# Weights of a hybrid decoder trunk, laid out in the order in which the kernel reads them

## The chip, the cores and the metric

The kernel runs on one core of one Trainium2 chip. The metric is the device time of one execution in microseconds (us); the number to beat is the median of several runs.

## The reference

Two layers, each a conditioned mixer over a sequence of 1024 tokens of width 1024, all in float32. The conditioning vector `c` is turned into shift, scale and gate by `w_mod`; the normalised and modulated input goes through one wide projection `w_in`, whose columns feed three groups of heads (sliding-window attention, retention, gated linear attention); the gated results are joined and go through `w_out`.

```python
def hybrid_layer(x, c_act, positions, w_mod, b_mod, pre_gain, post_gain, w_in, sinks,
                 gla_gate_w, gla_gate_b, gla_norm_gain, w_out):
    mod = c_act @ w_mod + b_mod                      # w_mod: 1024 x 3072
    shift, scale, gate = jnp.split(mod[:, None, :], 3, axis=-1)
    h = rms_norm(x, pre_gain) * (1.0 + scale) + shift
    proj = h @ w_in                                  # w_in: 1024 x 3088
    (aq, ak, av, ag, rq, rk, rv, rg, gq, gk, gv, gg, ga) = jnp.split(proj, IN_SPLITS, axis=-1)
    ...
    y = jnp.concatenate([a_out, r_out, g_out], axis=-1) @ w_out   # w_out: 1024 x 1024
    return x + gate * rms_norm(y, post_gain)
```

## The kernel before

The sequence lies in eight tiles of 128 tokens. The projections run in float32 accuracy as three passes over a high and a low part of each operand, so every weight block is loaded once and then split into two tiles: the high part by a copy (ScalarE, ACT, or VectorE, DVE) and the low part by a subtraction (DVE or GpSimd, POOL). The split is what the lines 529 to 535 do, under the names `arena<-st` in the profile.

**Weights of the projections.** `w_in` is cut into 12 units of 256 columns (`gg`, `rg`, `rq`, `rk`, `rv`, `gqk`, `gv`, `kv`, `aq0`, `aq1`, `ag0`, `ag1`), `w_out` of layer 0 into four (`o0` to `o3`). `load(l, name)` fetches a unit in four transfers: each brings, for 128 partitions, two pieces of 256 columns (1 KB each) into one of five `st` buffers (256 KB). The contraction index of such a piece is `(k p)`: partition p of piece k is row 128 k + p of the weight, so neighbouring partitions read neighbouring rows. With the unit `gg` go the 16 columns `ga`, in one transfer of 64 KB made of pieces of 64 bytes (line 541). For layer 1's output the four units are replaced by blocks of 128 x 512, loaded by `sw_load` in one piece of 2 KB per partition.

**Weights of the conditioning.** `mod_first` computes shift and scale of layer 0 at the very start: for each half of the columns (`hh`) it loads two tiles `wm` of 8 x 512 columns per partition, one for shift (summed by TensorE, PE) and one for scale (summed by DVE, line 328), in transfers of two, two, two, one and one `k`. Here the contraction index is `(p k)`: partition p has rows 8 p to 8 p + 7. All other thirds are done by `mod_third`, one transfer of 128 x 512 for each k (line 361), in the same `st` buffers.

**The order of the work.** PE's order is written out by the source: generators are queued as jobs and released against a planned clock `clk[0]` with due times from the table `L`; this planned clock does not look at the layout of a transfer. For the other engines and the DMA queues the order of instructions is settled when the kernel is built (line 1703 leaves only PE to the source). Every engine then runs its list in order. Nearly all weight transfers are issued from SyncE's queue (SP). The x tiles of the first two tokens' tiles (`xk`) are issued from ACT's queue, the next two (`mx`) from SP after the second half's `wm`, the later ones (`pre_first`, `t<-in_x`) after that; constants come with `cload` (line 234), called below them in the source.

The host side, `kernel()`, already permutes columns of `w_in` and rows of `w_out`.

Of the kernel before, what the change touches and what calls it, by code (L numbers as in the profile page):

```python
# [17 lines left out]
P = 128  # L18
D = 1024
S = 1024  # L20
DEPTH = 2
NT = S // P
NP_ = NT // 2
KT = D // P
# [4 lines left out]
GQ, GK, GV, GG, GA = 2304, 2432, 2560, 2816, 3072  # L29
D_IN = 3088  # L30

UNITS = [
    ("gg", GG), ("rg", RG),
    ("rq", RQ), ("rk", RK), ("rv", RV),
    ("gqk", GQ), ("gv", GV),
    ("kv", AK), ("aq0", AQ), ("aq1", AQ + 256),
    ("ag0", AG), ("ag1", AG + 256),
    ("o0", 0), ("o1", 256), ("o2", 512), ("o3", 768),
]
COLS = dict(UNITS)  # L40

LOG_CLAMP = -24.0

# [48 lines left out]
def trunk(ctx: ExitStack, tc: tile.TileContext, ins, cst, out):  # L92
    nc = tc.nc
    V, A, G, T = nc.vector, nc.scalar, nc.gpsimd, nc.tensor
    x_in, c_in, pos_in, w_mod, b_mod, pre_g, post_g, w_in, sinks, gw_in, gb_in, gn_in, w_out = [
        ins[n] for n in _INS
    ]

# [21 lines left out]
    def small(w, dt=F32):  # L120
        return gp.tile([P, w], dt, tag="sm", name=nm("sm"), bufs=BS)

    def mm():
        return ps.tile([P, 512], F32, tag="mm", name=nm("mm"), bufs=MMB)
# [26 lines left out]
    def dma(k, dst, src):  # L151
        {"S": nc.sync, "A": A, "P": G}[EN[k]].dma_start(dst, src)
# [35 lines left out]
    def flag(name, lat=0.0):  # L188
        flags[name] = clk[0] + lat
# [100 lines left out]
    def mod_tile(l, j):  # L290
        modc[(l, j)] = cp.tile([P, KT], F32, name=nm(f"mod{j}"), tag=f"mod{j}")

    def mod_first(rws, between):
        wv = w_mod[0].rearrange("(p k) n -> p k n", k=KT)
        for j in range(2):
            mod_tile(0, j)
        rc = []
        shift, gain = modc[(0, 0)], modc[(0, 1)]

        def finish(hh, row, acc):  # L300
            pc = mm()
            for b in range(4):
                mult(pc[:, 4 + b:5 + b], acc[:, b * P:(b + 1) * P], ones[:, 0:1], True, True)
            for b in range(4):
                mult(pc[:, b:b + 1], row[0:1, b * P:(b + 1) * P], ones[0:1, 0:1], True, True)
            ks = slice(4 * hh, 4 * hh + 4)
            col = small(4)
            V.tensor_tensor(col, pc[:, 4:8], rc[1][:, ks], ALU.add)
            V.scalar_tensor_tensor(gain[:, ks], col, 1.0, rc[1][:, 8 + 4 * hh:12 + 4 * hh], ALU.add, ALU.mult)
            V.tensor_tensor(shift[:, ks], pc[:, 0:4], rc[0][:, ks], ALU.add)  # L310
            flag(("modh", 0, hh), 0.0)

        late = None
        for hh in range(2):
            wm = [wp.tile([P, KT, 512], F32, name=nm("wm")) for _ in range(2)]
            acc = t2()
            row = gp.tile([1, 512], F32, tag="acc", name=nm("row"), bufs=1)
            pm = mm()
            for k0, k1 in ((0, 2), (2, 4), (4, 6), (6, 7), (7, 8)):
                for j in range(2):  # L320
                    c0 = j * D + 512 * hh
                    nc.sync.dma_start(wm[j][:, k0:k1, :], wv[:, k0:k1, c0:c0 + 512])
            between(hh, -1)
            for k in range(KT):
                if k == 0:
                    V.tensor_scalar(acc, wm[1][:, k], c_act[:, k:k + 1], None, ALU.mult)
                else:
                    mark[2] = V.scalar_tensor_tensor(acc, wm[1][:, k], c_act[:, k:k + 1], acc, ALU.mult, ALU.add)  # L328
                mult(pm[0:1, :], c_act[:, k:k + 1], wm[0][:, k], k == 0, k == KT - 1)
                if hh == 0 and k == 3:  # L330
                    rc.extend(mod_rows_t(r_) for r_ in rws)
                if late is not None and k == FIN:
                    pump()
                    finish(0, *late)
                    pump()
                between(hh, k)
            A.activation(row, pm[0:1, :], AF.Copy)
            if hh == 0:
                late = (row, acc)
        finish(1, row, acc)  # L340
        pump()

    def mod_third(l, j):
        wv = w_mod[l].rearrange("(p k) n -> p k n", k=KT)
        if j < 2:
            mod_tile(l, j)
            rows = mod_rows(l, j)
            yield lat("mod1", l)
            rc = mod_rows_t(rows)
        else:  # L350
            res = cp.tile([P, D], F32, name=nm("modg"), tag="modg")
            modg[l] = res
        for hh in range(2):
            c0 = j * D + 512 * hh
            acc = gp.tile([P, 512], F32, tag="acc", name=nm("acc"), bufs=1)
            if j == 2:
                G.memset(acc, 0.0)
                nc.sync.dma_start(acc[0:1, :], b_mod[l:l + 1, c0:c0 + 512])
            for k in range(KT):
                wt = stage()  # L360
                dma("lwm", wt, wv[:, k, c0:c0 + 512])
                if k == 0 and j < 2:
                    V.tensor_scalar(acc, wt, c_act[:, k:k + 1], None, ALU.mult)
                else:
                    V.scalar_tensor_tensor(acc, wt, c_act[:, k:k + 1], acc, ALU.mult, ALU.add)  # L365
                yield lat("mod2", l)
            yield lat("mod3", l)
            pm = aux()
            if j < 2:
                for b in range(4):  # L370
                    mult(pm[:, b:b + 1], acc[:, b * P:(b + 1) * P], ones[:, 0:1], True, True)
                mod_cols(l, j, hh, pm, rc)
                if j == 0:
                    flag(("modh", l, hh), lat("mod4", l))
            else:
                mult(pm, allones, acc, True, True)
                gain = stage()
                nc.sync.dma_start(gain, post_g[l:l + 1, 512 * hh:512 * hh + 512].to_broadcast((P, 512)))
                V.tensor_tensor(res[:, 512 * hh:512 * hh + 512], pm, gain, ALU.mult)
            yield lat("mod5", l)  # L380
        flag(("mod", l, j), lat("mod6", l))
# [127 lines left out]
    def load(l, name, first=None):  # L509
        if l >= DEPTH:  # L510
            return
        c0 = COLS[name]
        src = w_out[l] if name[0] == "o" else w_in[l]
        wt = unit(l, name)
        sv = src.rearrange("(k p) n -> p k n", p=P)

        def issue(kc):
            st = stage().rearrange("p (k n) -> p k n", k=2)
            dma("lw", st, sv[:, 2 * kc:2 * kc + 2, c0:c0 + 256])
            return (st,)  # L520

        def conv(kc, st):
            hi, lo = (wt[:, a, 2 * kc:2 * kc + 2, 0:256] for a in range(2))
            if name[0] == "o" and kc == 3:
                A.activation(hi, st, AF.Copy, scale=gnc[:, l:l + 1])
                V.scalar_tensor_tensor(lo, st, gnc[:, l:l + 1], f(hi), ALU.mult, ALU.subtract)
            else:
                if first == 0:
                    A.activation(hi, st, AF.Copy)
                elif first == 1:  # L530
                    V.tensor_copy(hi, st)
                else:
                    copy(f"whi{kc}", hi, st)
                e = G if first == 0 or name[0] == "o" and kc == 2 else eng(f"wlo{kc}")
                e.tensor_tensor(lo, st, f(hi), ALU.subtract)  # L535
            if kc == 3:
                if name == "gg":
                    gt = wt[:, :, :, 256:272]
                    st = t1()
                    sg = st[:, 0:128].rearrange("p (k n) -> p k n", k=KT)  # L540
                    nc.sync.dma_start(sg, sv[:, :, GA:GA + 16])
                    A.activation(gt[:, 0], sg, AF.Copy)
                    V.tensor_tensor(gt[:, 1], sg, f(gt[:, 0]), ALU.subtract)
                flag(("w", l, name))

        for kc in range(KT // 2):
            if first is not None:
                conv(kc, *issue(kc))
            else:
                request(l, 1, lambda kc=kc: issue(kc), lambda st, kc=kc: conv(kc, st))  # L550
# [6 lines left out]

    def sw_load(k, i, j):
        st = stage()
        r = P * (4 * i + k)  # L560
        dma("lw", st, w_out[DEPTH - 1, r:r + P, 512 * j:512 * j + 512])
        return st

    def sw_split(name, k, st, key):
# [1099 lines left out]
    while jobs:  # L1664
# [10 lines left out]
FIN = 1  # L1675

_INS = ["x", "c", "positions", "w_mod", "b_mod", "pre_norm_gain", "post_norm_gain", "w_in", "attn_sinks",
        "gla_gate_w", "gla_gate_b", "gla_norm_gain", "w_out"]


# [26 lines left out]
```

## Time and profile before

| | |
|---|---|
| median of 3 runs | 1006.1 us (1002.45 to 1006.14) |
| profiled execution, its span from first to last instruction | 1008.9 us |
| PE busy in it | 975.4 us (97%) |
| DVE, ACT, POOL busy | 684.5, 408.8, 234.4 us |
| bytes moved by DMA | 148.73 MB, 147 GB/s on average |
| share of the 16 DMA engines' time, SP's queue (q1) and ACT's (q10) | 45.3%, 2.6% |

The profile page gives busy time, shares and groups of instructions; other views give the chain of waits, the timeline of an engine, and a table of chosen stretches of time with the busy time of each engine, the granted TensorE clock, the busy share of the DMA engines and the rate at which they moved data. Times within the execution are counted from its first instruction. A tile's name stands for all its buffers.

### The profile page before, as it was taken

How to read it: one execution, taken by the hardware profiler on the slowest of the kernel's cores; microseconds unless marked ns; L12 is line 12 of the kernel's file. 1: busy time of each engine (PE TensorE's matmuls, PEld its weight loads, DVE VectorE, ACT ScalarE, POOL GpSimd, SP SyncE). 2: the span in 40 equal slices, each digit the busy share in tenths (PEclk: the TensorE clock that was granted, in tenths of full speed). 3: DMA queues.
4: the chain of work that ended last, by engine and by line, in shares of the span. 5: the costliest groups of instructions: out<-in, count | busy, mean ns of one | idle time of the engine just before them, and what ended most of it. 6: DMA issues, size and time to landing. Idle time of an engine off the chain costs nothing.

```text
span 1008.9 us, 19610 instructions
## 1 busy us (share of the span) xinstructions
PE 975.4 (97%) x7137; PEld 829.5 (82%) x7137; DVE 684.5 (68%) x1680; ACT 408.8 (41%) x1152; POOL 234.4 (23%) x275
## 2 busy tenths in 40 slices
PE   5899999899999999999999999999999999999897
PEld 1499999888998777778889999998899877777785
DVE  3789857757666778564578275785666577566876
ACT  2476311223322656632465232123332256663321
POOL 2310001223320234330112000113332034544100
PEclk8899999999999999999999999999999999999999
DMA  9942513623326355577655251353132434378883
GB/s 293 308 137 76 173 45 100 170 81 96 96 74 199 89 149 163 171 239 244 214 157 173 64 158 32 108 150 100 41 104 85 125 90 130 112 236 249 265 263 140
DMA packets 129836, 148.73 MB, mean 147 GB/s; under 512 B 14046, under 2 KB 94152, under 8 KB 129740
## 3 DMA queue, kind: packets, MB, share of 16 engines
q1 hardware_dynamic: 124044, 137.92, 45.3%
q10 hardware_dynamic: 5696, 9.56, 2.6%
q8 instruction: 56, 0.92, 0.4%
q14 instruction: 40, 0.33, 0.1%
HBM read 109.17 MB, written 36.18 MB: 144 GB/s over the span
## 4 chain that ended last, share of the span: by engine, by line
PE 80%; DVE 8%; DMA 7%; issue 2%; POOL 1%; ACT 1%; SPq 0%; POOLq 0%; DVEq 0%; ACTq 0%
PE mm L163 61%; PE aux L163 14%; PE aux L178 5%; DMA st<-in_w_in_dram 2%; DMA st<-in_w_out_dram 1%; POOL sm L638 1%; DMA xk<-in_x_dram 1%; DMA wm<-in_w_mod_dram 1%; DMA t<-aoS 1%; DVE arena L535 1%; DMA st<-in_w_mod_dram 1%; DMA t<-sgS 1%; DVE t L328 0%; DVE st L572 0%; DMA mixF<-t 0%
## 5 line engine op out<-in xcount | busy, mean ns | idle before, releaser
L163 PE MATMUL mm<-arena 128*128 128x256 f32 (+2 forms) x1824 | 299.2, 318 | 1.8 <-ACT arena L707 1.8
L163 PE MATMUL mm<-arena,arena 128*128 128x256 f32 (+2 forms) x1824 | 300.7, 318 | 0.0
L163 PEld LDWEIGHTS mm<-arena 128*128 128x128 f32 x1824 | 254.6, 191 | 26.5 <-issue 4.1
L163 PEld LDWEIGHTS mm<-arena,arena 128*128 128x128 f32 x1824 | 254.1, 189 | 25.5 <-issue 4.6
L638 POOL TENSOR_TENSOR sm<-sm,mhalf 128x1 f32<-128x1 f32 (+1 forms) x64 | 56.1, 877 | 347.0 <-DVE sm L637 328.6
L163 PE MATMUL mm<-arena,mx 128*128 128x512 f32 (+1 forms) x564 | 132.4, 392 | 2.9 <-ACT kept L1335 2.9
L163 PEld LDWEIGHTS mm<-arena,mx 128*128 128x128 f32 x564 | 103.1, 191 | 27.1 <-ACT kept L1335 3.3
L147 ACT ACTIVATE t<-aux 128x256 f32<-128x256 f32 (+2 forms) x124 | 55.7, 467 | 76.1 <-PE aux L178 64.8
L147 ACT ACTIVATE arena<-st 128x512 fp32r<-128x512 f32 x94 | 56.1, 626 | 59.1 <-DMA st<-in_w_in_dram 21.4
L535 POOL TENSOR_TENSOR arena<-st,arena 128x512 fp32r<-128x512 f32 x31 | 43.2, 1395 | 138.9 <-ACT arena L147 100.9
L926 POOL TENSOR_TENSOR smx<-smx,sm 128x512 f32<-128x512 f32 x32 | 36.1, 1127 | 124.3 <-DVE sm L925 116.1
L535 DVE TENSOR_TENSOR arena<-st,arena 128x512 fp32r<-128x512 f32 x77 | 59.5, 795 | 6.1 <-ACT arena L147 4.1
L922 ACT ACTIVATE smx<-smx,sm 128x129 f32<-128x129 f32 x128 | 49.9, 392 | 28.4 <-DVE sm L919 28.4
L178 PE MATMUL aux<-c_ident,t 128*128 128x128 f32 (+1 forms) x292 | 48.8, 285 | 7.6 <-DVE t L669 7.2
L365 DVE SCALAR_TENSOR_TENSOR acc<-st,c_act,acc 128x512 f32<-128x512 f32 x60 | 45.5, 759 | 12.6 <-DMA st<-in_w_mod_dram 12.1
L178 PEld LDWEIGHTS aux<-c_ident,t 128*128 128x128 f32 (+1 forms) x292 | 35.4, 145 | 15.2 <-DVE t L669 9.0
L701 ACT ACTIVATE t<-aux,mod,mod 128x128 f32<-128x128 f32 x68 | 25.9, 458 | 43.8 <-DVE t L1242 18.2
L970 ACT ACTIVATE t<-aux 128x256 f32<-128x256 f32 x32 | 12.3, 383 | 75.5 <-PE aux L163 63.4
L163 PEld LDWEIGHTS aux<-t,mx 32*128 32x128 f32 (+1 forms) x896 | 39.5, 187 | 3.8 <-issue 2.1
L163 PE MATMUL aux<-t,mx 32*128 32x32 f32 (+1 forms) x896 | 40.7, 273 | 0.0
L917 DVE COPY_PREDICATED smx<-c_curmask,aux 128x256 f32<-128x256 int32 x64 | 25.5, 447 | 18.8 <-ACT smx L147 15.3
L1242 DVE SCALAR_TENSOR_TENSOR t<-t,sm,t 128x512 f32<-128x512 f32 x32 | 24.0, 779 | 18.6 <-DMA t<-in_x_dram 11.9
(220 smaller groups left out, 1384.3 us busy)
## 6 DMA issues: line engine op xcount, KB each, us to landing
st<-in_w_in_dram SPq DMA_DIRECT2D x96, 256.0 KB, 3.1
st<-in_w_mod_dram SPq DMA_DIRECT2D x64, 256.0 KB, 3.3
st<-in_w_out_dram SPq DMA_DIRECT2D x52, 256.0 KB, 3.8
mx<-mixS SPq DMA_DIRECT2D x20, 512.0 KB, 6.2
mixS<-t SPq DMA_DIRECT2D x72, 128.0 KB, 2.3
wm<-in_w_mod_dram SPq DMA_DIRECT2D x12, 512.0 KB, 8.0
t<-in_x_dram SPq DMA_DIRECT2D x24, 256.0 KB, 4.8
t<-tabS SPq DMA_DIRECT2D x16, 256.0 KB, 3.7
```

Source lines behind the costliest of these rows:

```text
L147: A.activation(dst, src, AF.Copy)
L163: T.matmul(dst, lhsT, rhs, start=start, stop=stop)
L178: T.transpose(dst, src, idn)
L365: V.scalar_tensor_tensor(acc, wt, c_act[:, k:k + 1], acc, ALU.mult, ALU.add)
L535: e.tensor_tensor(lo, st, f(hi), ALU.subtract)
L638: G.tensor_tensor(r, r, mhalf[:, :w], ALU.pow)
L701: A.activation(hf[:, ks], at[kt], AF.Identity, scale=gain, bias=shift)
L917: V.copy_predicated(sv, curmask.unsqueeze(1).to_broadcast((P, 2, P)), pv[:, :, n // P - 1, :])
L922: A.activation(sm[:, h, :], sm[:, h, :], AF.Exp, bias=mx[:, h:h + 1], accum_out=sums[:, h:h + 1])
L926: eng("pn").tensor_tensor(sm[:, :, 0:128], sm[:, :, 0:128], rs.unsqueeze(2).to_broadcast((P, 4, P)), ALU.mult)
L970: A.activation(sq, po, AF.Square)
L1242: V.scalar_tensor_tensor(xt[j], yg[j], r, xt[j], ALU.mult, ALU.add)
```

## The change

The host writes `w_in`, `w_out` and `w_mod` in the blocks in which the kernel reads them. `w_in` becomes (layer, unit, partition, k, 256 columns), so that a partition's two pieces of a transfer lie side by side (2 KB), and the `ga` columns become an input of their own, `w_ga`, with 512 bytes per partition. `w_out` of layer 0 gets the same form; that of layer 1 becomes an input `w_last` of 128 x 512 blocks. `w_mod` becomes (layer, third, half, partition, k, 512 columns), so that a transfer of two k reads 4 KB per partition. The same bytes go to the same tiles in the same number of transfers; the table `L`, the buffers and the engines are unchanged.

```diff
+NIN = 12
+ORDER = {n: i if i < NIN else i - NIN for i, (n, _) in enumerate(UNITS)}
...
     def mod_first(rws, between):
-        wv = w_mod[0].rearrange("(p k) n -> p k n", k=KT)
...
                 for j in range(2):
-                    c0 = j * D + 512 * hh
-                    nc.sync.dma_start(wm[j][:, k0:k1, :], wv[:, k0:k1, c0:c0 + 512])
+                    nc.sync.dma_start(wm[j][:, k0:k1, :], w_mod[0, j, hh, :, k0:k1, :])
...
     def mod_third(l, j):
-        wv = w_mod[l].rearrange("(p k) n -> p k n", k=KT)
...
-                dma("lwm", wt, wv[:, k, c0:c0 + 512])
+                dma("lwm", wt, w_mod[l, j, hh, :, k, :])
...
     def load(l, name, first=None):
-        c0 = COLS[name]
         src = w_out[l] if name[0] == "o" else w_in[l]
         wt = unit(l, name)
-        sv = src.rearrange("(k p) n -> p k n", p=P)
+        sv = src[ORDER[name]]
...
-            dma("lw", st, sv[:, 2 * kc:2 * kc + 2, c0:c0 + 256])
+            dma("lw", st, sv[:, 2 * kc:2 * kc + 2, :])
...
-                    nc.sync.dma_start(sg, sv[:, :, GA:GA + 16])
+                    nc.sync.dma_start(sg, w_ga[l])
...
     def sw_load(k, i, j):
         st = stage()
-        r = P * (4 * i + k)
-        dma("lw", st, w_out[DEPTH - 1, r:r + P, 512 * j:512 * j + 512])
+        dma("lw", st, w_last[j, 4 * i + k])
...
+    def blocks(a, starts, n):
+        return np.stack([a[:, :, c:c + n].reshape(-1, KT, P, n).transpose(0, 2, 1, 3) for c in starts], 1)
+
+    inputs["w_in"] = blocks(w_in, [c for _, c in UNITS[:NIN]], 256)
+    inputs["w_ga"] = blocks(w_in, [GA], 16)[:, 0]
+    inputs["w_out"] = blocks(w_out, [c for _, c in UNITS[NIN:]], 256)[:DEPTH - 1]
+    inputs["w_last"] = w_out[DEPTH - 1].reshape(KT, P, 2, 512).transpose(2, 0, 1, 3)
+    inputs["w_mod"] = np.asarray(inputs["w_mod"]).reshape(DEPTH, P, KT, 3, 2, 512).transpose(0, 3, 4, 1, 2, 5)
```

More of the change, by code (lines that the diff above doesn't have):

```diff
@@ L94, in trunk @@
     V, A, G, T = nc.vector, nc.scalar, nc.gpsimd, nc.tensor
-    x_in, c_in, pos_in, w_mod, b_mod, pre_g, post_g, w_in, sinks, gw_in, gb_in, gn_in, w_out = [
+    x_in, c_in, pos_in, w_mod, b_mod, pre_g, post_g, w_in, sinks, gw_in, gb_in, gn_in, w_out, w_ga, w_last = [
         ins[n] for n in _INS
@@ L1677 @@
 _INS = ["x", "c", "positions", "w_mod", "b_mod", "pre_norm_gain", "post_norm_gain", "w_in", "attn_sinks",
-        "gla_gate_w", "gla_gate_b", "gla_norm_gain", "w_out"]
+        "gla_gate_w", "gla_gate_b", "gla_norm_gain", "w_out", "w_ga", "w_last"]
 def kernel(**inputs):
@@ L1690 @@
     inputs = dict(inputs)
-    inputs["w_in"] = np.asarray(inputs["w_in"])[:, :, icols]
-    inputs["w_out"] = np.asarray(inputs["w_out"])[:, orows, :]
+    w_in = np.asarray(inputs["w_in"])[:, :, icols]
+    w_out = np.asarray(inputs["w_out"])[:, orows, :]
+    def blocks(a, starts, n):
[5 more added lines that the diff above has]
+    inputs["w_mod"] = np.asarray(inputs["w_mod"]).reshape(DEPTH, P, KT, 3, 2, 512).transpose(0, 3, 4, 1, 2, 5)
     for name in _INS:
```

## The prediction

> **What bounds the kernel now.** I read the page first: the span, then the engines' shares.
>
> ```profile
> core 0: 1008.9 us, clock 0.986
> PE 975.4 (97%) x7137; PEld 829.5 (82%) x7137; DVE 684.5 (68%) x1680; ACT 408.8 (41%) x1152; POOL 234.4 (23%) x275
> ```
>
> TensorE (PE) is busy 975.4 of 1008.9 us. The change alters no matmul, so it can only shorten the 33.5 us in which PE stands still, plus matmuls that run at a lowered clock. Where those microseconds lie is read from the table of 25 us stretches; its columns are the stretch, its length, then busy time and instruction count of PE, weight load, DVE, ACT and POOL, then granted clock, DMA share and GB/s.
>
> ```profile
> 0.00:25.00 25.00, 13.07 (x33) 4.62 (x34) 8.81 (x24) 6.27 (x13) 5.24 (x14) 0.86 0.90 292
> 25.00:50.00 25.00, 20.86 (x94) 11.81 (x92) 18.24 (x38) 10.85 (x28) 8.00 (x8) 0.87 0.91 307
> ...
> 175.00:200.00 25.00, 21.91 (x176) 20.73 (x176) 19.06 (x51) 8.51 (x17) 6.66 (x5) 0.98 0.57 160
> ...
> 675.00:700.00 25.00, 22.34 (x144) 19.47 (x144) 13.53 (x34) 7.96 (x19) 7.71 (x9) 1.00 0.46 138
> ...
> 925.00:950.00 25.00, 22.11 (x88) 17.46 (x87) 20.38 (x35) 10.00 (x21) 6.46 (x6) 0.93 0.76 239
> ```
>
> PE idles 11.9 us in the first stretch, 4.1 in the second, then 3.1, 2.7 and 2.9: 24.7 of the 33.5 us. The first two have the DMA engines at 0.90 and 0.91: the start is bound by transfers. The other three are single stalls. Next I read the chain of waits in order of time, columns start, length, what.
>
> ```profile
> 2.88 7.05 DMA wm<-in_w_mod_dram
> 9.95 7.26 DMA xk<-in_x_dram
> 17.22 3.26 DMA st<-in_w_in_dram
> ...
> 24.10 3.52 PE mm L163 x4
> ...
> 28.97 1.27 DVE arena L543
> ...
> 159.72 2.47 DMA st<-in_w_in_dram
> ...
> 192.30 5.80 DMA st<-in_w_in_dram
> ...
> 668.95 3.09 DMA st<-in_w_in_dram
> ...
> 673.98 3.61 DMA st<-in_w_in_dram
> ...
> 678.79 4.17 DMA st<-in_w_in_dram
> ...
> 915.43 4.71 DMA st<-in_w_out_dram
> ```
>
> So w_in transfers stand on the chain five times after the start, 19.1 us together. The stall near 196 us shows how one reaches PE, in the timelines of ACT and of PE:
>
> ```profile
> 198.19 0.63 ACT L147 ACTIVATE arena<-st 128x512 fp32r<-128x512 f32 x1 [2.87 <-DMA st<-in_w_in_dram]
> 198.72 0.85 ACT L147 ACTIVATE t<-aux 128x256 fp32r<-128x256 f32 x2
> ...
> 199.62 0.58 PE L163 MATMUL aux<-t 64*128 64x128 f32 x2 [3.09 <-ACT t L147]
> ```
>
> ACT runs its list in order. It waits 2.87 us for a weight block to land, the copy behind it (wanted by retention's matmul) goes late, and PE stands 3.09 us. The block is not the one PE needs next; it is merely ahead in ACT's list.
>
> **The change part by part.** Which transfers change is read from the page's DMA issues (count, KB each, us to landing) and the durations of their issue on SP (min/median/max).
>
> ```profile
> st<-in_w_in_dram SPq DMA_DIRECT2D x96, 256.0 KB, 3.1
> st<-in_w_mod_dram SPq DMA_DIRECT2D x64, 256.0 KB, 3.3
> wm<-in_w_mod_dram SPq DMA_DIRECT2D x12, 512.0 KB, 8.0
> t<-in_w_in_dram SPq DMA_DIRECT2D x2, 64.0 KB
> ...
> L152 SPq DMA_DIRECT2D st<-in_w_in_dram x96: 367/383/2046, 14.4 to 828.7; - x96
> L152 SPq DMA_DIRECT2D st<-in_w_mod_dram x64: 327/333/1082, 67.3 to 671.0; - x64
> ```
>
> The 96 w_in transfers, and 16 of w_out for layer 0, go from two 1 KB runs per partition to one of 2 KB. The 12 wm transfers of 512 KB go from two 2 KB runs to one of 4 KB. The two w_ga transfers (64 KB) go from eight 64 B runs to one of 512 B. The 64 w_mod transfers of mod_third, the eight single-k wm transfers and layer 1's w_out already read 2 KB per partition: only their addresses change. No transfer is added or moved in the source, none gets a new wait, and the tiles are filled as before, so what reads them costs the same.
>
> What a longer run saves is not a row; I work it out from two stretches in which the DMA engines are saturated, the first while layer 0's rg (1 KB runs) lands, the second while wm and x (2 KB runs) land.
>
> ```profile
> 37.00:39.00 2.00, 1.30 (x11) 1.29 (x11) 1.25 (x2) 0.64 (x2) 0.00 (x0) 1.00 1.06 353
> 28.00:34.00 6.00, 6.00 (x26) 2.60 (x25) 4.99 (x8) 1.85 (x6) 3.02 (x2) 0.98 1.04 391
> ```
>
> Rate over share gives 353/1.06 = 333 GB/s at 1 KB and 391/1.04 = 376 GB/s at 2 KB. One of 16 engines thus takes 1024 x 16 / 333 = 49.2 ns for a 1 KB run and 87.1 ns for a 2 KB run: a fixed part of 2 x 49.2 - 87.1 = 11.3 ns per run, and 37.9 ns per KB. These are estimates from mixed stretches; the fixed part could be anything from 0 to some 15 ns. A 256 KB transfer at 1 KB is 16 runs per engine and becomes 8: 8 x 11.3 = 0.09 us saved. A 512 KB wm transfer goes from 16 runs to 8 as well: 0.09 us. The w_ga transfer is 64 runs of 13.7 ns (0.88 us), then 8 of 30.3 ns (0.24 us): 0.63 us saved.
> The Trainium skill (DMA: Bandwidth & Descriptors, section Specifications) gives 512 B as the least transfer for line rate. By that rule 1 KB runs have nothing to gain, only w_ga would; the rates of 333 and 376 GB/s here disagree, and I go by them.
>
> Also, the issue with two runs takes 383 ns on SP, the issue with one 333: 0.05 us each, 112 x 0.05 = 5.6 us of SP in all. SP is not on the chain except through the transfers it issues, so this counts only where a transfer does.
>
> At the start, if all savings reached the end, they would be 12 x 0.09 + 4 x 0.09 (gg) + 0.63 = 2.07 us. The least is what lies ahead of the x tiles: the first half's six wm transfers, 0.54 us. From 17 us on the chain leaves the transfers for PE (24.10) and DVE (28.97, the w_ga conversion) and comes back to wm only through DVE work, so part of the saving is hidden; I take 1.3 us, the middle.
> Later, each of the five w_in pieces loses its own 0.09 + 0.05 = 0.14 us, and up to two more 0.09 where neighbours land just before it: 0.7 to 1.6 us for five, I take 1.1. What is late next there is PE's own queue, and PE is full, so the gain passes on.
> The w_out pieces near 915 us are layer 1's, with 2 KB runs already: 0. Cheaper transfers elsewhere land ahead of conversions that have slack: 0; if that slack is not there, it would show as pieces of the chain, and it doesn't.
>
> Sum: -2.4 us (-1.2 to -3.7), so 1006.5 for the profiled execution's 1008.9. That execution stands 2.8 us above the median of 1006.1, so the forecast is 1006.1 - 2.4 = 1003.7 us, with 1002.4 to 1004.9 as this case's own range. That is a real gain, but under 0.5% (5 us), which is about what a measurement of this kernel can tell from no change.
>
> **The rivals.** *B, the start gains more: the scattered reads themselves are slow.* The start's mean rate and the clock:
>
> ```profile
> 15.00:20.00 5.00, 0.72 (x4) 0.72 (x5) 1.93 (x5) 1.44 (x4) 0.00 (x0) 0.80 1.00 335
> ...
> 2.00:28.00 26.00, 16.07 (x36) 4.99 (x37) 8.47 (x22) 6.64 (x14) 5.79 (x6) 0.81 0.98 320
> 18.00:28.00 10.00, 7.84 (x21) 3.73 (x22) 4.60 (x10) 2.98 (x6) 5.24 (x5) 0.50 1.05 334
> ```
>
> At share 0.98 only 320 GB/s move, although most of it is 2 KB runs that reach 376 later. If layout is the cause, 26 us x 320 = 8.3 MB take 22.1 us at 376: -3.9. PE's 7.84 us at clock 0.50, from 18 us on, follow a stretch in which it was busy 0.72 of 5 us; with a shorter standstill, none to half of those, 0 to -3.9 us. With the later 1.1 us: -5.0 to -8.9, or 997 to 1001. Against it: the same wm layout does reach 376 in its second half, so the slowness may belong to the first transfers after a start.
>
> *C, slower: the order of the other engines' lists moves.* Only PE's list is in source order. SP's rows show that lists are rearranged when the kernel is built: the source issues the x tiles before the constants, while the trace has
>
> ```profile
> 37.21 0.34 SPq L234 DMA_DIRECT2D c_causal<-cst_causal_dram  x1
> ...
> 40.81 7.70 SPq L718 DMA_DIRECT2D t<-in_x_dram  x8
> 48.56 0.42 SPq L234 DMA_DIRECT2D c_qdec<-cst_qdec_dram  x1
> ```
>
> If the new shapes change what that ordering takes a transfer to cost, a conversion can move ahead of a copy that PE wants, as at 196 us, on ACT or DVE. Price: 3.09 us for each new place. Two make 6.2 - 2.4 = +3.8, still within 0.5%; from three on (+6.9, 1013 us) it is slower. Against: bytes, tiles and waits are the same, and w_ga is the one transfer whose shape changes much. A new order may also lift one of today's three stalls (-3 on top of -2.4: 1001).
>
> *D, slower: equal steps between partitions.* Today w_in's partitions lie 12,352 bytes apart; afterwards 8 KB, and w_mod's 16 KB. Transfers that read 2 KB every 8 KB exist already:
>
> ```profile
> ma<-mixS SPq DMA_DIRECT2D x12, 256.0 KB, 4.8
> a<-mixS SPq DMA_DIRECT2D x6, 256.0 KB, 6.6
> ```
>
> They land in 4.8 and 6.6 us against w_in's 3.1. If the step is the reason, five pieces pay at least 1.7 us each: +8.5, 1014 us. It decides from about 1 us each. Against: these are issued in twos and threes behind other transfers, and wm, at a step of 96 KB, reaches 376 GB/s.
> The Trainium skill (DMA: Bandwidth & Descriptors, section Latency and other measured facts) has row pitches of 2 MiB and more slowing copies and 512 KiB near full rate. By that row 8 and 16 KB cost nothing; no run here shows the large pitches.
>
> *E, nothing of note:* the cost of a run is all bytes, or the two runs are still sent apart. Then only w_ga's 0.6 us go: 1005.5.
>
> **How the numbers follow.** Forecast 0.34, B 0.30, C 0.26, D 0.05, E 0.05. Faster by over 0.5%: B's 0.30, 0.03 of the forecast's upper tail and 0.05 of C where the new order is lucky: 0.38. Slower: 0.19 of C and D's 0.05: 0.24. The rest, 0.31 + 0.02 + 0.05 = 0.38, is within 0.5%. Cases of both signs hold most of the chance; the likeliest one's own range is 1002.4 to 1004.9. The range for 8 in 10 reaches down through B to 997 and up to 1012, which leaves out most of slow C, D and a little of B.
>
> **What the changed profile would show.** Packets first:
>
> ```profile
> DMA packets 129836, 148.73 MB, mean 147 GB/s; under 512 B 14046, under 2 KB 94152, under 8 KB 129740
> ```
>
> If runs join, 112 x 128 = 14,336 packets go with w_in and w_out, 12 x 128 = 1,536 with wm, 2 x 896 = 1,792 with w_ga: 112,172 remain, some 65,500 of them under 2 KB. w_in's issue should fall from 383 to about 333 ns and its landing from 3.1 to about 3.0 us. PE's busy time should stay at 975 us and its idle time fall by 2 to 3 us, over half of it before 50 us. B is right if the stretch from 2 to 28 us moves over 360 GB/s; C if SP, ACT or DVE run in another order and a stall of some 3 us stands at a new place; D if w_in's landing rises; E if packets or landing stay. The forecast is wrong above all if the order changes or if the start shortens by more than 3 us.

## The result, and the profile after

The changed kernel takes 1001.6 us (median of 20 runs, 998.6 to 1005.5); the kernel before, in 20 runs beside it, 1005.4 us (1001.0 to 1009.5). The ratio is 0.996, 95% interval 0.9947 to 0.9972: 4.0 us less (2.8 to 5.3). The gain is real, and at 0.4% it is under 0.5% (5 us) as forecast, though the interval reaches a little beyond. On PE, DVE, ACT, POOL and SP the instructions stand in the same order as before.

The profiled execution of the changed kernel: its span with the granted clock, and the engines' shares from the page.

```profile
core 0: 1003.6 us, clock 0.989
PE 972.6 (97%) x7137; PEld 827.5 (82%) x7137; DVE 683.7 (68%) x1680; ACT 409.0 (41%) x1152; POOL 234.7 (23%) x275
```

Its table of stretches, with the same columns as in the prediction:

```profile
0.00:25.00 25.00, 13.78 (x33) 4.77 (x34) 8.89 (x24) 6.23 (x13) 5.62 (x14) 0.88 0.87 306
25.00:50.00 25.00, 21.36 (x103) 13.78 (x102) 19.14 (x40) 11.63 (x31) 8.66 (x9) 0.85 0.84 296
175.00:200.00 25.00, 23.18 (x183) 21.51 (x183) 17.98 (x50) 6.74 (x14) 6.67 (x5) 1.00 0.61 185
675.00:700.00 25.00, 24.22 (x183) 20.53 (x182) 14.23 (x40) 8.64 (x23) 7.71 (x9) 1.00 0.29 90
925.00:950.00 25.00, 21.28 (x85) 16.73 (x84) 19.03 (x35) 7.26 (x16) 2.61 (x4) 0.93 0.79 249
2.00:28.00 26.00, 16.78 (x39) 5.23 (x39) 8.69 (x23) 7.53 (x16) 6.08 (x7) 0.87 0.95 342
```

PE idles 31.0 us where it idled 33.5, and its busy time fell by 2.8 us although it runs the same matmuls. (Single profiles scatter by as much: the unchanged kernel, profiled again as e12 below, idles 29.6 us and is busy 970.8.) By stretch the idle time is now 11.2, 3.6, 1.8, 0.8 and 3.7 us where it was 11.9, 4.1, 3.1, 2.7 and 2.9. The stall of layer 0 shrank; the one near 940 us did not. Layer 1's idle time is not the single stall that the prediction took it for: in the timeline of the kernel before it is 1.28 us behind ACT, then 1.01 and 0.37 behind DVE. In the changed kernel it begins ahead of 675 us, so the stretch that holds all of it is 650 to 700 us: 2.68 us before, 1.45 now.

The w_in transfers on the changed kernel's chain of waits:

```profile
14.99 5.12 DMA st<-in_w_in_dram
...
190.13 4.60 DMA st<-in_w_in_dram
...
662.87 3.21 DMA st<-in_w_in_dram
...
668.02 3.17 DMA st<-in_w_in_dram
...
672.39 3.21 DMA st<-in_w_in_dram
```

The stall near 196 us in its timelines of ACT and of PE:

```profile
194.81 0.63 ACT L149 ACTIVATE arena<-st 128x512 fp32r<-128x512 f32 x1 [1.45 <-DMA st<-in_w_in_dram]
...
196.25 0.71 PE L165 MATMUL aux<-t 64*128 64x128 f32 x8 [1.82 <-ACT t L149]
```

The same copy waits for the same block, but 1.45 us instead of 2.87, and PE stands 1.82 us instead of 3.09. What happens behind that stall is seen in the stretch from 200 to 205 us, here of the kernel before:

```profile
200.00:205.00 5.00, 5.00 (x20) 4.01 (x18) 0.76 (x2) 0.00 (x0) 0.15 (x1) 0.50 0.61 166
```

and of the changed kernel:

```profile
200.00:205.00 5.00, 5.00 (x32) 4.43 (x32) 2.25 (x7) 1.11 (x4) 1.43 (x2) 1.00 0.10 33
```

After the long stall PE is "busy" all the time, but at a granted clock of 0.50: 20 matmuls end in 5 us instead of 32. In these two profiles part of the busy time went there. Last, the changed kernel's packets and w_in's landing (page), then the row of w_in's issues on SP, whose first three numbers are least, median and longest in ns:

```profile
DMA packets 112172, 148.73 MB, mean 148 GB/s; under 512 B 11998, under 2 KB 63688, under 8 KB 112076
...
st<-in_w_in_dram SPq DMA_DIRECT2D x96, 256.0 KB, 3.7
```

```profile
L154 SPq DMA_DIRECT2D st<-in_w_in_dram x96: 327/333/1345, 14.4 to 821.5; - x96
```

The runs joined, to the packet; the issue fell to 333 ns; the median landing rose to 3.7 us.

### The profile page after: what moved, and what is told of

Read it like the earlier page. It is cut to its first block, busy times and chain, and to the rows that moved or that the text cites. A ratio compares the mean times of both kernels' runs of the same rounds, so it can differ in the third digit from the quotient of the medians.

```text
span 1003.6 us, 19610 instructions
## 1 busy us (share of the span) xinstructions
PE 972.6 (97%) x7137; PEld 827.5 (82%) x7137; DVE 683.7 (68%) x1680; ACT 409.0 (41%) x1152; POOL 234.7 (23%) x275
## 2 busy tenths in 40 slices
DMA packets 112172, 148.73 MB, mean 148 GB/s; under 512 B 11998, under 2 KB 63688, under 8 KB 112076
## 4 chain that ended last, share of the span: by engine, by line
PE 80%; DMA 8%; DVE 7%; issue 2%; POOL 1%; ACT 1%; SPq 1%; ACTq 0%; POOLq 0%; DVEq 0%
PE mm L165 62%; PE aux L165 14%; PE aux L180 5%; DMA st<-in_w_in_dram 2%; DMA st<-in_w_last_dram 1%; POOL sm L635 1%; DMA xk<-in_x_dram 1%; DMA a<-mixS 1%; DMA t<-aoS 1%; DMA t<-mixF 1%; DVE arena L533 1%; DVE t L328 0%; SPq L154 0%; DMA t<-in_x_dram 0%; DMA t<-xs 0%
```

## The experiments

Each kernel was timed beside runs of the kernel before on the same chip; ratios are against it.

### Which of the three weights

**e1, only w_mod**, and later **e10**, the same kernel again:

```diff
-                    nc.sync.dma_start(wm[j][:, k0:k1, :], wv[:, k0:k1, c0:c0 + 512])
+                    nc.sync.dma_start(wm[j][:, k0:k1, :], w_mod[0, j, hh, :, k0:k1, :])
...
-                dma("lwm", wt, wv[:, k, c0:c0 + 512])
+                dma("lwm", wt, w_mod[l, j, hh, :, k, :])
```

> Only w_mod is laid out in blocks; w_in and w_out are read as before. Theory (a run has a fixed cost of some 11 ns, so 4 KB runs in wm save 0.09 us per transfer): 12 x 0.09 = 1.1 us at most, 0.5 to 1 us of it reaching the end, ratio 0.999 to 0.9995, first projection's start 0.5 us earlier. Rival (the start is slow because wm's partitions lie 96 KB apart): the whole gain of the start, 1.1 us or more, is here, and the stretch from 2 to 28 us moves over 335 GB/s. The stall near 196 us stays in both.

> The kernel with w_mod alone laid out, measured a second time on other executions. If its 2 us over the kernel before are real, the ratio is 1.001 to 1.003 again; if they were chance, it is 0.999 to 1.000, since the start is held by the landing of wm and a run of 4 KB saves little.

Measured 1.0021 (1.0002 to 1.0039), then 1.0015 (0.9998 to 1.0031), where e1's theory expected a small gain. The part of the start's gain that belongs to wm, at most 1.1 us, is not there; gg and w_ga are as before in this kernel, so it says nothing of them.

**e2, only w_in and w_ga:**

```diff
-            sv = src.rearrange("(k p) n -> p k n", p=P)
+            sv = w_in[l][ORDER[name]]
...
-                    nc.sync.dma_start(sg, sv[:, :, GA:GA + 16])
+                    nc.sync.dma_start(sg, w_ga[l])
```

> Only w_in and w_ga are laid out; w_mod and w_out are read as before. Theory: it holds most of the change's 3.9 us, 2 to 3.5 us (ratio 0.9965 to 0.998), through the w_in pieces of the chain: the stall of PE near 196 us falls from 3.1 us to about 1.8 and the 5 us at half clock behind it vanish. Rival (the gain is spread over all three weights by bytes): half of it, 2 us, and the stall stays as it was.

Measured 0.9969 (0.9951 to 0.9986), 3.1 us of the 4.0. Its piece of the chain of waits near 190 us, then PE's stall behind it in the timeline:

```profile
191.02 4.12 DMA st<-in_w_in_dram
```

```profile
196.67 0.71 PE L165 MATMUL aux<-t 64*128 64x128 f32 x8 [1.34 <-ACT t L149]
```

**e3, only w_out:** `sv = w_out[l][ORDER[name]]` and `w_last`, the rest as before.

> Only w_out is laid out, for layer 0 in 2 KB runs and for layer 1 in blocks of 128 x 512 that were 2 KB runs before. Theory: no piece of the chain gets cheaper, 0 us, ratio 0.999 to 1.001. Rival (neighbouring rows make even 2 KB runs faster): 1 us or more between 890 and 950 us.

Measured 0.9997 (0.9981 to 1.0013): nothing, as the prediction's 0 for w_out says.

### Which property of the layout

**e4, the blocks with short runs.** The same blocks, but k outside the partition, so that a transfer's two pieces lie 128 KB apart for w_in (1 KB each) and 256 KB apart for wm (2 KB each), and w_ga is read in pieces of 64 B again:

```diff
-        return np.stack([a[:, :, c:c + n].reshape(-1, KT, P, n).transpose(0, 2, 1, 3) for c in starts], 1)
+        return np.stack([a[:, :, c:c + n].reshape(-1, KT, P, n) for c in starts], 1)
...
-        sv = src[ORDER[name]]
+        sv = src[ORDER[name]].rearrange("k p n -> p k n")
...
```

> All three weights in blocks as in the change, but inside a block k lies outside the partition, so a w_in or w_out transfer still reads two runs of 1 KB per partition, wm two runs of 2 KB and w_ga eight of 64 B; a block's rows lie next to each other. It keeps the locality and gives up the longer runs. Theory (run length is the cause): 0 us, ratio 0.999 to 1.001, packets as before (129,836), w_in's issue 383 ns. Rival (locality of the rows is the cause): 3 to 4 us faster, as the change.

**e5, each transfer one unbroken piece.** The same runs, but partitions 2 KB (w_in) and 4 KB (wm) apart instead of 8 and 16 KB:

```diff
-            dma("lw", st, sv[:, 2 * kc:2 * kc + 2, :])
+            dma("lw", st, sv[kc])
...
+        return np.stack([a[:, :, c:c + n].reshape(-1, KT // 2, 2, P, n).transpose(0, 1, 3, 2, 4) for c in starts], 1)
...
```

> As the change, but the blocks go one step further: what one transfer reads lies in one piece of memory (partitions 2 KB apart for w_in and w_out, 4 KB for wm), where the change leaves 8 KB and 16 KB between partitions. Theory (run length and short stalls): the same runs, so the same time as the change, ratio 0.995 to 0.997. Rival (the step between partitions costs something, or nearness of the rows is what helped): 1 us or more below the change, ratio under 0.995.

**e6, w_in in runs of 512 B**, four to a partition and transfer, all else as in the change:

```diff
-            dma("lw", st, sv[:, 2 * kc:2 * kc + 2, :])
+                dma("lw", st.rearrange("p k (c n) -> p (k c) n", c=2), sv[4 * kc:4 * kc + 4].rearrange("q p n -> p q n"))
```

> The change with w_in alone cut finer: a transfer reads four runs of 512 B per partition from four packed blocks, instead of one of 2 KB. Theory (a fixed part of 11 ns per run): 24 more runs per engine, 0.27 us more per w_in transfer, five of them on the chain and longer stalls near 190 and 670 us: 1.5 to 4 us over the change, ratio 0.9975 to 1.0. Rival (nearness of the rows, not run length): as the change, 0.996.

Measured: e4 0.9981 (0.9967 to 0.9996), e5 0.9955 (0.9935 to 0.9975), e6 1.000 (0.998 to 1.0019). The packets of e6 on its page, the stall near 196 us in the timeline of e6, and the same in that of e5:

```profile
DMA packets 149036, 148.73 MB, mean 148 GB/s; under 512 B 11998, under 2 KB 112840, under 8 KB 148940
```

```profile
197.79 0.72 PE L165 MATMUL aux<-t 64*128 64x128 f32 x8 [2.86 <-ACT t L149]
```

```profile
196.05 0.71 PE L165 MATMUL aux<-t 64*128 64x128 f32 x8 [1.77 <-ACT t L149]
```

With w_in's run cut from 2 KB to 512 B, and nothing else of the change taken back, the whole gain is lost and the stall is back. This also brings w_in's partitions from 8 KB to 512 B apart, but the step between partitions is not the cause: e5 shortens it as well, keeps the 2 KB, and equals the change. So the run's length is the cause. e4 came out between its theory (0.999 to 1.001) and its rival: 1 KB runs in blocks stand between; how much of its 0.19% comes from the nearness of the rows stays open, since its interval and those of the unchanged kernel and of the change touch.

### Is the start held by its low clock

**e7** adds 25 matmuls whose result nobody uses in PE's standstills of the changed kernel's start, to keep the clock up. (It also moved one copy in ACT's list by two places.)

```diff
+    def warm(bank, n, c=0):
+        for _ in range(n):
+            T.matmul(bank[:, c:c + P], ident, ident, start=True, stop=True)
...
+            if hh:
+                warm(pc, 4, P)
...
+            if t == 0:
+                warm(x, 16)
...
+                if l == 0 and t == 0 and name == "gg":
+                    warm(pg, 5, 300)
```

> The change, with 25 matmuls more in PE's list that compute nothing of use (identity times identity into columns that are overwritten or unread): 16 ahead of the first transposes near 15 us, 4 ahead of the second half's sums near 36 us, 5 ahead of the first projection near 39 us, that is in PE's standstills of the start. Theory (half clock follows a standstill of PE): the half clock of 18 to 28 us and 39 to 46 us shrinks or goes, the mean clock rises from 0.991 to 0.994 or more, and 1.5 to 3 us go on top of the change, ratio 0.993 to 0.9945. Rival (the start is set by the transfers and the clock costs nothing there): ratio 0.996 as the change, or above if the added matmuls come too late.

Measured 0.9979 (0.996 to 0.9998), 2 us above the change. Its stretch from 18 to 28 us, then two rows of its PE timeline:

```profile
18.00:28.00 10.00, 7.65 (x42) 4.06 (x41) 5.81 (x10) 3.20 (x6) 7.58 (x7) 1.00 1.02 388
```

```profile
33.38 1.02 PE L165 MATMUL mm<-wm,c_act 128*1 128x512 f32 x2 [1.28 <-DMA wm<-in_w_mod_dram]
...
48.50 1.97 PE L180 MATMUL aux<-c_ident,t 128*128 128x128 f32 x8 [2.03 <-DVE t L672]
```

The clock is full from 18 to 28 us, where the changed kernel has 0.66 and the prediction's row of the kernel before 0.50, and yet PE arrives at 48.50 us, as the change does (48.53, below). At 33 us it waits for wm, at 48 us for DVE. So no cost of the half clock is to be seen at the start. Why e7 lies above the change stays open; their intervals overlap.

### Does the half clock behind the stall cost

**e8** puts such matmuls (10 in layer 0, 6 in layer 1) into the kernel before, ahead of retention's last scores, where PE stands near 196 and 675 us; **e11** puts the same into the changed kernel. (In both, one multiplication by the causal mask, in layer 1, moved in DVE's list by three places.)

```diff
+        if t == NT - 1:
+            warm(sp[0], (10, 6)[l])
```

> The kernel before, with added matmuls of no use (10 in layer 0, 6 in layer 1) in PE's list just where it stood at 196.5 to 199.6 us and near 680 us, ahead of retention's last score matmuls. No transfer changes. Theory (the late weight block costs a stall, and the stall costs half clock behind it): PE no longer stands for over 1.5 us there, the half clock behind it vanishes, mean clock up by 0.001 to 0.002 and 1 to 2.5 us less, ratio 0.9975 to 0.999. Rival (the half clock has another cause): ratio 1.0, and half clock still at 200 to 205 us in some executions.

> The change, with the added matmuls of no use in PE's standstills before retention's last score matmuls (10 in layer 0, 6 in layer 1), and none at the start. Theory (stall and half clock behind it): the change already cut those stalls to 1.8 us or less, with half clock only in some executions, so 0.5 to 1.5 us less than the change, ratio 0.9945 to 0.9955. Rival (added matmuls come as late as they help): 0.996 to 0.997.

Measured: e8 0.9979 (0.9962 to 0.9997), e11 0.9995 (0.9979 to 1.001). PE's timeline in e8, the stretch behind its stall, and PE's timeline in e11:

```profile
193.20 2.39 PE L649 MATMUL aux<-c_ident 128*128 128x128 f32 x20
...
196.81 0.71 PE L163 MATMUL aux<-t 64*128 64x128 f32 x8 [1.22 <-ACT t L147]
```

```profile
195.00:210.00 15.00, 13.79 (x86) 11.84 (x85) 5.18 (x15) 3.48 (x9) 3.97 (x5) 1.00 0.32 106
```

```profile
194.96 2.39 PE L646 MATMUL aux<-c_ident 128*128 128x128 f32 x20
...
197.28 0.72 PE L165 MATMUL aux<-t 64*128 64x128 f32 x8
```

In e8 the filling and the rest of the stall take 2.39 + 1.22 = 3.6 us, so the filling lies inside the stall and is free; the clock behind it stays at 1.00, and the kernel is 2.1 us faster (0.3 to 3.8) with no weight moved. One profile can't show that the filling kept the clock up, since e12 below has 1.00 there without it. The mean clock of all executions does: 0.9912 over the 12 of e8, 0.9891 over the 33 of the kernel before beside them. In e11 the stall is only some 1.8 us: the filling is longer, PE's next matmul waits for nothing, and comes late. e11 lies 0.0035, or 3.5 us, above the change. The expectation that it would gain was wrong: its mean clock, 0.9908, is that of the change (0.9907), so the filling won no clock. Of the loss the trace accounts for 0.6 us here (2.39 less the 1.82 of the changed kernel's stall) and for 1.2 us in layer 1, where 1.50 of filling and 0.25 of waiting stand in place of a wait of 0.51; the rest stays open.

### Does w_mod's layout cost something

**e9** is the change without its part for w_mod (both lines of e1 back, and `inputs["w_mod"]` as before).

> The change without w_mod's part: w_in, w_ga and w_out in blocks, w_mod read as before. Theory (w_in carries the gain, w_mod's longer runs at the start reach nothing): as the change, ratio 0.996. Rival (w_mod's layout alone really costs 2 us, as its first run had it): 2 us below the change, ratio 0.994.

Measured 0.9951 (0.9933 to 0.9969), median 999.1 us in 6 runs, the lowest of all. Its chain of waits near 190 us, then PE's timeline behind it:

```profile
188.28 3.66 DMA st<-in_w_in_dram
```

```profile
193.47 0.72 PE L165 MATMUL aux<-t 64*128 64x128 f32 x8 [0.87 <-ACT t L149]
```

e1, e10 and e9 point the same way: w_mod in blocks brings nothing and may cost a microsecond or two. But e9's interval overlaps the change's, so a version that beats the change isn't proven.

### How far one profile can be trusted

**e12** is the kernel before, unchanged.

> The kernel before, unchanged, measured against itself: the ratio tells what the comparison makes of nothing (0.999 to 1.001), and the profile is a second execution, to tell what belongs to the kernel from what belongs to one execution: first projection's matmuls and the stall near 196 us may differ by 1 to 3 us from the first profile.

Measured 0.9998 (0.9978 to 1.0017). Its span, four of its stretches, its piece of the chain near 190 us, and PE's stall behind that in the timeline:

```profile
core 0: 1000.4 us, clock 0.992
```

```profile
0.00:25.00 25.00, 13.34 (x34) 4.69 (x35) 8.81 (x24) 6.27 (x13) 5.64 (x14) 0.86 0.91 300
25.00:50.00 25.00, 21.64 (x107) 14.14 (x106) 19.69 (x41) 12.16 (x32) 9.20 (x9) 0.86 0.92 309
...
2.00:28.00 26.00, 16.34 (x43) 5.45 (x43) 9.16 (x23) 7.58 (x16) 6.65 (x7) 0.87 0.98 327
195.00:210.00 15.00, 13.23 (x81) 11.48 (x82) 5.21 (x15) 3.47 (x9) 4.00 (x5) 1.00 0.34 108
```

```profile
190.15 5.10 DMA st<-in_w_in_dram
```

```profile
196.77 0.71 PE L163 MATMUL aux<-t 64*128 64x128 f32 x8 [2.39 <-ACT t L147]
```

The same kernel gave spans of 1008.9 and 1000.4 us in two profiles, the second below that of the changed kernel. Here the start idles 15.0 us without any change (16.1 in the first profile, 14.9 in the changed kernel), and the clock behind the stall of 2.39 us stays full. So a comparison of the first two profiles alone would have credited the change with both.

## Why the prediction was right, and where its sizes were off

The sign, a gain under 0.5% and the mechanism of the later term were right: joined runs make w_in land sooner where ACT's ordered list waits for it, and PE starts sooner by that. The forecast was 2.4 us, 4.0 were measured (2.8 to 5.3), just outside the forecast's own range of 1.2 to 3.7. Both terms were mis-sized and a third was missing; that the sum came as near as it did is luck, since a start term that the runs don't show stands in it for a later gain that was put too low. To see past the scatter of single executions, the readings of the eleven profiles without added matmuls stand side by side: PE's idle time in three stretches, the granted clock from 195 to 210 us, and the length of the w_in piece of the chain near 190 us.

| w_in's runs | kernel | idle 0-50 us | idle 175-200 | idle 650-700 | clock 195-210 | piece near 190 |
|---|---|---|---|---|---|---|
| 1 KB, old | before | 16.1 | 3.09 | 2.68 | 0.77 | 5.80 |
| | e12 | 15.0 | 2.39 | 2.38 | 1.00 | 5.10 |
| | e1 | 15.3 | 2.78 | 2.93 | 0.77 | 5.49 |
| | e10 | 16.1 | 2.90 | 3.34 | 0.89 | 5.61 |
| | e3 | 14.8 | 2.16 | 2.08 | 1.00 | 4.86 |
| 512 B | e6 | 14.4 | 2.86 | 2.54 | 0.89 | 5.53 |
| 1 KB, blocks | e4 | 14.5 | 2.35 | 2.62 | 1.00 | 5.06 |
| 2 KB | after | 14.9 | 1.82 | 1.45 | 1.00 | 4.60 |
| | e2 | 14.8 | 1.34 | 1.40 | 1.00 | 4.12 |
| | e5 | 14.7 | 1.77 | 1.62 | 0.89 | 4.55 |
| | e9 | 14.4 | 0.87 | 1.79 | 1.00 | 3.66 |

**The later term, 1.1 us, was too small.** The stall of layer 0 fell from 2.66 us (mean of the five old ones) to 1.45 (mean of the four with 2 KB), layer 1's stretch (three short stalls, not the single one of the prediction) from 2.68 to 1.57: 2.3 us together. The prediction charged a piece of the chain with its own 0.09 us, 0.05 of issue and up to two neighbours' 0.09. The piece near 190 us shrank by 1.1 us (means 5.37 and 4.23), several times that, and the two groups don't overlap, in the piece or in the stall. It was the step "each piece loses its own runs' fixed cost" that failed. In every one of these profiles SP issues three more w_in transfers in the 5.5 us ahead of this one; with those and the issue the prediction's own price comes to some 0.4 us, still too little. In what way the other transfers in flight there take part, no run separates.

**A term was missing: the clock behind the stall.** Three of the five old profiles have the half clock after it, one of the four new ones. The mean clock of that stretch rose from 0.886 to 0.973, which over 15 us is 2.6 us less at 0.50 (0.087 x 15 / 0.5); at that clock 20 matmuls end for 32, as in the rows from 200 to 205 us, so three eighths of those 2.6 us were lost: about 1.0 us. It can also be timed, since PE's list is the same in all eleven kernels. After the stall PE runs on from its row at 199.62 us to this row, in the kernel before and in the changed kernel (there from 196.25):

```profile
214.67 2.63 PE L163 MATMUL mm<-arena 128*128 128x256 f32 x21
```

```profile
208.51 2.63 PE L165 MATMUL mm<-arena 128*128 128x256 f32 x21
```

That is 15.05 and 12.26 us for the same matmuls. Where the table has a clock of 1.00 the way takes 12.25 to 12.27 us, at 0.89 some 13.8, at 0.77 15.05 and 15.17; the means of the old and the new kernels are 13.70 and 12.65, again 1.05 us apart.

Three of five against one of four could be chance. The mean clocks of whole executions, of which there are many more, speak against that: 0.9892 over 109 executions of the kernel before (with e12's twelve, at 0.9900), 0.9866 to 0.9890 in e1, e10, e3 and e6, but 0.9907 over the 20 of the change and 0.9901 to 0.9912 in e2, e5 and e9; e4 lies between with 0.9894. A step of 0.0015 over 1004 us is 3.0 us less at 0.50, by the same three eighths some 1.1 us. It need not all lie behind this one stall: in layer 1 the five old kernels have a clock of 1.00 from 650 to 700 us. The prediction looked for this only at the start. e8 tests it without a change of weights: a higher clock, 2.1 us gained. The two terms make 3.3 us, against e2's 3.1 and the change's 4.0.

**The start term, 1.3 us, was not shown.** e1 and e10 contain all of its wm part and are no faster. Idle time before 50 us is 15.0 us on average with the old wm (before, e12, e3, e2, e9) and 15.1 with 4 KB runs (after, e1, e10, e5, e6). PE's arrival at the eight transposes near 48 us, in the timelines of the kernel before, of e12 and of the changed kernel:

```profile
49.63 1.09 PE L178 MATMUL aux<-c_ident,t 128*128 128x128 f32 x8 [1.52 <-DVE t L669]
```

```profile
47.99 1.09 PE L178 MATMUL aux<-c_ident,t 128*128 128x128 f32 x8 [0.89 <-DVE t L669]
```

```profile
48.53 1.09 PE L180 MATMUL aux<-c_ident,t 128*128 128x128 f32 x8 [0.65 <-DVE t L666]
```

The unchanged kernel alone moves by 1.6 us. The waits at this point are for DVE, as the prediction said of the part that is hidden; it took the middle of its bounds where the lower end, or less, was right. w_ga's 0.63 us may be there: sorted by w_ga, the idle time before 50 us is 15.3 us on average with runs of 64 B (before, e12, e1, e10, e3, e4) and 14.6 with 512 B (after, e2, e5, e6, e9). But the groups overlap, and gg's runs differ between them too, so it is not shown.

**The signs.** Packets (112,172) and issue (333 ns) came as forecast; the 65,500 under 2 KB were 63,688, since the 1,792 of w_ga that vanish lie under 2 KB too. PE's busy time did not stay at 975, which fits the clock, and its idle time fell by 2.5 us as forecast; but neither these nor "over half before 50 us" can be read from one pair of profiles, as e12 shows (busy 970.8, idle 29.6). "Landing about 3.0" missed: it is 3.2 to 4.1 us in the six profiles with 2 KB runs and 3.1 to 3.6 in the six with the old w_in. The median over 96 transfers, most of which nobody waits for, doesn't carry the effect; why it moved stays open.

**The rivals.** B asked for over 360 GB/s from 2 to 28 us: it is 342 in the change, but 327 in e12 and 352 in e8, which read all weights as before, so the rate there moves without any change of layout; and in e7 the clock it wanted to save is full from 18 us on, without PE arriving sooner. C falls with the unchanged lists. D's sign, a landing that rises, did appear, but its mechanism is refuted by e5: steps of 2 and 4 KB give 0.9955, those of 8 and 16 KB 0.996. E allowed 0.6 us; 4.0 were measured, with the packets joined.

The Trainium skill (DMA: Bandwidth & Descriptors, section Specifications) gives 512 B as the least transfer for line rate. By that rule e6 and the change should take the same time; they are at 1.000 and 0.996. The measurement decides: in this kernel, runs above 512 B were still worth 0.4%.

## What to carry to other kernels

A layout that lengthened the runs of weight transfers paid here where an engine that works through an ordered list waited for such a transfer, not by the bytes or packets saved in all: look for the few blocks on the chain of waits, and add what a long stall does to the clock behind it. Test each weight by itself; here one of three brought nearly the whole gain, and one perhaps cost some of it. Before microseconds are credited to a change of 0.4%, profile the unchanged kernel again, read the same stall in several profiles, and compare the mean clocks of all executions.

## What the runs showed of the hardware

The granted clock drops behind stalls that are quite short: here e1, whose PE stood 2.78 us, in its timeline and in the stretch after it.

```profile
197.33 1.23 PE L163 MATMUL aux<-t 64*128 64x128 f32 x8 [2.78 <-ACT t L147]
```

```profile
195.00:210.00 15.00, 12.67 (x62) 10.90 (x63) 4.01 (x12) 2.81 (x7) 2.69 (x3) 0.77 0.39 120
```

The eight matmuls behind the stall take 1.23 us instead of 0.71. At this place stalls of 2.16 to 2.39 us (e3, e4, e12) left the clock at 1.00, those of 2.78 to 3.09 us brought it to 0.77 or 0.89 over the 15 us, that is to half clock for some 6.9 or 3.3 of them. But the stall's length alone doesn't settle it: e5 has 0.89 after 1.77 us, e7 after 2.00, and in layer 1 the clock from 675 to 700 us is 0.93 with a stall of 1.40 us in e2 and 1.00 with one of 2.58 in e1:

```profile
675.13 0.99 PE L165 MATMUL aux<-t 64*128 64x128 f32 x8 [1.40 <-ACT t L149]
```

```profile
679.56 0.71 PE L163 MATMUL aux<-t 64*128 64x128 f32 x8 [2.58 <-ACT t L147]
```

The Trainium skill (TensorE: Matmul & The Clock Gate, Part 1) puts the fall to half clock after an idle window of about 3.4 us; these traces have it behind shorter stalls.

Keeping the clock up is not a gain in itself: e7 has the highest mean clock of all, 0.994, and is no faster than the change.
